# Folding 1/rms into the last down group's activations, and moving the norm's ones-products behind other products

## The chip, the core and the metric

One core of a Trainium2 chip runs the whole program. Its engines run side by side, each with a queue of its own that is worked off in order: TensorE (PE, with the weight loads as PEld), VectorE (DVE), ScalarE (ACT), GpSimd (POOL) and SyncE (SP, which issues most loads). The metric is the device time of one execution in microseconds, as the median of several runs. TensorE's clock has two levels, 1.2 and 2.4 GHz, and the profile's granted clock says which share of the full one a stretch had.

## What is computed

A two-layer encoder over 512 positions of width 1024, in float32. The reference, cut to what matters here:

```python
for i in range(2):
    h = h + 0.5 * swiglu(rmsnorm(h, ffn1_norm[i]), ...)        # (silu(x Wg) * (x Wu)) Wd, inner width 2816
    u = rmsnorm(h, mix_norm[i]) @ w_in[i]                      # feeds attention, mLSTM, Fourier mixing
    h = h + concat(y_mla, y_mlstm, y_fnet) @ w_out[i]
    h = h + 0.5 * swiglu(rmsnorm(h, ffn2_norm[i]), ...)
    e = rmsnorm(p[i] @ ple_w_proj[i], ple_post_norm[i])        # embedding, 256 wide, per layer
    h = h + sigmoid(rmsnorm(h, ple_gate_norm[i]) @ ple_w_gate[i]) * e
out = rmsnorm(h, final_norm)
```

## The kernel before

The state `h` lies transposed in SBUF as 8 tiles of 128 channels by 512 positions. Every matrix product is made of three TensorE products, since each float32 operand is split into a rounded part and a rest (`mm3`, lines 161 to 163: `xh` or `ah` with `whi`, `xl` or `al` with `whi`, `xh` or `ah` with `wlo`). ScalarE casts the rounded part (L134, L376), VectorE subtracts the rest (L131). Weights arrive in 512 KB tiles through SP's queue.

The factor 1/rms of a norm is not multiplied into the input of a product. `Stage.high` and `Stage.low` (L305, L312) make `xh` and `xl` from `h` times the gain alone and sum the squares on the way (`sqacc`, L199). The factor follows later in two forms: `Norm.tok` (L209) multiplies `sqacc` by a column of ones on TensorE, four small products, and VectorE makes 1/rms from it in a dozen small steps (`rtok`); `Norm.bc` (L245) spreads `rtok` over the partitions with four transposes on TensorE, and ScalarE copies it out as `rbc` (L247). Results are multiplied by `rbc` afterwards.

- **Feed-forward.** The 22 inner tiles `u` are made one after the other; from the fifth on each takes seven smaller products (`p1` to `p7`, a Winograd form over halves of 256 positions). GpSimd multiplies the gate part `g1` (L546) and `g2` (L594) by `rbc`; ScalarE applies silu; `finish` multiplies `g2` by `c22` on GpSimd (L504); `p4` multiplies `g1` on VectorE (L582). The down-projection runs over groups of 5, 4, 4, 4 and 5 inner tiles; the last group's products stand at the end in an order written by hand. `flush` takes a finished output tile: VectorE multiplies it by `rbc` into `qa` (L603) and adds half of that to `h` (L604). In the last group `flush` also makes the next stage's `xh` and `xl`. The order in a feed-forward part is written out by hand on all engines.
- **Mixing.** `tokens` makes 96 products of width 272 (L718 to L720), 12 for each of the 8 channel tiles; `inT` follows with tiles of 512 (24 products each). TensorE's order is that of the program; the others are scheduled.
- **Embedding (`ple`).** 48 projection products (eight tiles `e`, copied out on ScalarE at L1302, squared and summed), then eight gate tiles of 24 products. `post` multiplies the eight `e` by their own norm (L1316). All engines are scheduled. In the second layer the gates are made in two halves of 256 positions, and their raw weights `gr` come through a ring of three buffers of its own (cast to `gh`, rest in `gl`, kept for both halves).

Of the kernel before, what the change touches and what calls it, by code (L numbers as in the profile page):

```python
# [14 lines left out]
ALU = mybir.AluOpType  # L15
# [9 lines left out]
NF = DFF // P  # L25
# [9 lines left out]
GROUPS = (5, 4, 4, 4, 5)  # L35
# [30 lines left out]
CH = {}  # L66
# [27 lines left out]
def trunk(ctx: ExitStack, tc, xT, pT, pos, W, gains, cst, dftc, out):  # L94
# [13 lines left out]
    V, S, G = nc.vector, nc.scalar, nc.gpsimd  # L108
# [219 lines left out]
    def ffn(l, cgu, cd, st, nxt, first=False):  # L328
# [2 lines left out]

        with tc.tile_pool(name="ap", bufs=1) as ap, tc.manual_schedule():
            items, clock = [], [0.0]

# [4 lines left out]
            def tile(tag, bufs, shape, dt=F32):  # L341
                return ap.tile([P] + shape, dt, tag=tag, name=tag, bufs=bufs)
# [4 lines left out]
            def qa():  # L347
                return tile("qa", 4, [T])

            def pw():  # L350
                return tile("pw", 6, [2, T], F32R)

            acts = {}

            def act(f):
# [140 lines left out]
            def small(tag):  # L496
                return tile(tag, 2, [H])

            h1, h2 = slice(0, H), slice(H, T)

            def finish(u):
                d = U[u]
                S.activation(d["g2"], d["g2"], AF.Silu)
                G.tensor_tensor(d["g2"], d["g2"], d["c22"], op=ALU.mult)  # L504
# [58 lines left out]
            def p7(u, after=None):  # L563
                def run():
                    d = U[u]
                    p = d["w", "S3"]
                    product(u, "B", p[:, 0], p[:, 1], "T3", False)
                    d["c22"] = small("c22")
                    S.copy(d["c22"], d["B"])
                    V.scalar_tensor_tensor(d["c22"], d["E"], -1.0, d["c22"], op0=ALU.mult, op1=ALU.subtract)  # L570
                    S.activation(d["g1"], d["g1"], AF.Silu)
                    if after is not None:
                        finish(after)

                return run, load(u, "S3", 0, "A11") + [(7.0, lambda: parts(u, "S3"))]
# [23 lines left out]
            pys = {}  # L599

            def flush(m, last):
                y = qa()
                V.tensor_tensor(y, pys.pop(m), st.rb, op=ALU.mult)  # L603
                V.scalar_tensor_tensor(h[:, m], y, 0.5, h[:, m], op0=ALU.mult, op1=ALU.add)  # L604
                if last:
                    nxt.high(m)
                    if m:
                        nxt.low(m - 1)
                    if m == NK - 1:
                        nxt.low(m)  # L610
# [51 lines left out]
            u, n = NF - 1, GROUPS[g]  # L662
# [21 lines left out]
    def mix(l, st, nxt):  # L684
        with tc.tile_pool(name="mp", bufs=1) as mp, tc.manual_schedule(engines={mybir.EngineType.PE}):
# [12 lines left out]
            def inT(i, tag="ps"):  # L698
                wh, wl = stream(l, CH["inT"] + i)
                pt = bank(tag)  # L700
                blocks(pt, wh, wl, st)
                return pt
# [4 lines left out]
            def tokens(first, n, width, after=()):  # L707

                per = -(-NK // n)
                pns = [bank() for _ in range(NT)]  # L710
                for k in range(NK):
                    if k % per == 0:
                        wh, wl = stream(l, first + k // per, width * min(per, NK - k))
                    b = slice((k % per) * width, (k % per + 1) * width)
                    for c in range(NT):
                        ts = slice(c * P, (c + 1) * P)
                        xh, xl, pn = st.hi[k][:, ts], st.lo[k][:, ts], pns[c][:, 0:width]
                        mm(pn, xh, wh[:, b], start=k == 0, stop=False)  # L718
                        mm(pn, xh, wl[:, b], start=False, stop=False)  # L719
                        mm(pn, xl, wh[:, b], start=False, stop=k == NK - 1)  # L720
                    if k in after:
                        after[k]()
                return pns
# [2 lines left out]
            V.memset(va[:, :, :, 64:65], 1.0)  # L726
            g16 = mp.tile([P, NT, 16], F32, name="g16")
            o = l * GW + _G["ifb"][0]
            pns = tokens(CH["inN"], 3, 272, {3: st.tok, 6: st.bc})
            pmx = [inT(j, "pm") for j in range(2)]  # L730
            for c in range(NT):
                V.scalar_tensor_tensor(g16[:, c], pns[c][:, 256:272], st.rt[:, c:c + 1], gv[:, o:o + 16],
                                       op0=ALU.mult, op1=ALU.add)
# [50 lines left out]
            qa, qb = t2("qa"), t2("qb")  # L784
# [67 lines left out]
            for j in range(2):  # L852
# [4 lines left out]
                for i in (0, 1, 3, 4):  # L857
                    a, b = max(0, 2 - i), T - max(0, i - 2)
# [25 lines left out]
            def maps(j):  # L884
# [12 lines left out]
                for c in range(NT):  # L897
# [10 lines left out]
            pns = tokens(CH["inF"], 2, 256, {3: lambda: rqs.append(nq.tok(st.rt)),  # L908
                                             6: lambda: rqs.append(nq.bc(rqs[0], MLA_SCALE))})
# [200 lines left out]
            kqs, qr, vs, probs, turned, pys = [], [], [], {}, {}, {}  # L1110
# [167 lines left out]
    def ple(l, st, nxt):  # L1278


        with tc.tile_pool(name="pp", bufs=2) as pp:
            raw = wp.tile([P, 2 * T], F32, tag="wraw", name="wraw", bufs=2)
            nc.sync.dma_start(raw, pT[l])
            ph = wp.tile([P, 2 * T], F32R, tag="whi", name="whi")
# [5 lines left out]
            for m in range(NK):  # L1290
                if m % 4 == 0:
                    wj = stream(l, CH["proj"] + m // 4)
                pe = bank("pm" if m % 2 else "ps")
                for j in range(2):
                    b = slice((2 * (m % 4) + j) * P, (2 * (m % 4) + j + 1) * P)
                    mm3(pe, wj[0][:, b], wj[1][:, b], ph[:, j * T:(j + 1) * T], pl[:, j * T:(j + 1) * T], j == 0, j == 1)
                if m == 3:
                    st.tok()
                if m == 6:
                    st.bc()  # L1300
                e = pp.tile([P, T], F32, tag="e", name="e", bufs=NK)
                S.copy(e, pe)  # L1302
                nm.add(e)
                es.append(e)
# [8 lines left out]
            def post(r):  # L1313
                rb = nm.bc(r)
                for i in range(NK):
                    V.scalar_tensor_tensor(es[i], es[i], gcol(l, "post", i), rb, op0=ALU.mult, op1=ALU.mult)  # L1316

            if nxt is not None:
                pgs = []
                for m in range(NK):  # L1320
                    gh, gl = stream(l, CH["gate"] + m)
                    pgs.append(bank("pm" if m % 2 else "ps"))
                    blocks(pgs[m], gh, gl, st)
                    if m == 0:
                        r = nm.tok()
                    if m == 1:
                        post(r)
                    for i in ((), (0, 1), (m,))[min(m, 2)]:
                        gate(i, pgs[i], slice(0, T))
                        nxt(i)  # L1330
                return
# [34 lines left out]
            for b in range(2):  # L1366
                pgs = []
                acc = pp.tile([P, T // 2], F32, tag="acc", name="acc")
                accs.append(acc)
                for m in range(NK):  # L1370
                    if b == 0:
                        raw = pp.tile([P, CHUNK], F32, tag="gr", name="gr", bufs=3)
                        nc.sync.dma_start(raw, W[l, CH["gate"] + m])
                        gw.append((pp.tile([P, CHUNK], F32R, tag="gh", name="gh", bufs=NK),
                                   pp.tile([P, CHUNK], F32R, tag="gl", name="gl", bufs=NK)))
                        split(*gw[m], raw)
                    pgs.append(bank("pm" if m % 2 else "ps")[:, 0:T // 2])
                    for k in range(NK):
                        kb = slice(k * P, (k + 1) * P)
                        mm3(pgs[m], gw[m][0][:, kb], gw[m][1][:, kb], st.hi[k][:, half[b]], st.lo[k][:, half[b]],  # L1380
                            k == 0, k == NK - 1)
                    if b == 0 and m == 1:
                        r = nm.tok()
                    if b == 0 and m == 2:
                        post(r)
                    if b == 1 and m == 2:
                        final_tok(0)
                    if b == 1 and m == 4:
                        final_out(0)
                    for i in ((), (), (0, 1, 2), (m,))[min(m, 3)]:  # L1390
                        gate(i, pgs[i], half[b])
                        sq = acc if i == 0 else pp.tile([P, T // 2], F32, tag="sq", name="sq")
                        S.activation(sq, h[:, i, half[b]], AF.Square)
                        if i < NK - 1:
                            S.activation(h[:, i, half[b]], h[:, i, half[b]], AF.Copy, scale=fg(i))
                        if i >= NK - 2:
                            sqs[b].append(sq)
                        elif i:
                            V.tensor_tensor(acc, acc, sq, op=ALU.add)
# [6 lines left out]
    st = stage(0, "ffn1")  # L1406
# [12 lines left out]
    for l in range(L):  # L1419
# [4 lines left out]
        st = stage(l + 1, "ffn1") if l + 1 < L else None  # L1424
# [132 lines left out]
```

## Time and profile before

| | us |
|---|---|
| median of 3 runs | 2092.74 (2091.53 to 2094.8) |
| profiled execution | 2091.12 |
| its span | 2089.3 |
| TensorE busy | 2008.6 (96%) |
| VectorE busy | 1567.7 (75%) |
| ScalarE busy | 1016.6 (49%) |
| GpSimd busy | 356.4 (17%) |
| mean granted clock of TensorE | 0.985 |

The span is the part of the execution that the trace covers; 1.8 us of the execution lie outside it. Shares are of the span. An engine counts as busy only for work, not for issuing loads or for waiting on a semaphore.

### The profile page before, as it was taken

The numbers are of one execution on the slowest core, as the hardware profiler recorded it, in microseconds if no ns is written. First come the engines' busy times: TensorE is split into PE (matmuls) and PEld (weight loads), VectorE is DVE, ScalarE is ACT, GpSimd is POOL, SyncE is SP. The second block draws the span as 40 slices with busy tenths as digits, with TensorE's granted clock in tenths as the row PEclk, the third lists the DMA queues.
The fourth block names the chain that finished last, engine by engine and source line by source line (L and its number), as shares of the span: only waits on it lengthen the run. The fifth ranks groups of instructions, "written<-read, shape, count | busy, mean of one in ns | idle before, by whom it ended". The sixth has DMA issues, their size and how long they took to land.

```text
span 2089.3 us, 31724 instructions
## 1 busy us (share of the span) xinstructions
PE 2008.6 (96%) x12216; PEld 1770.4 (85%) x12216; DVE 1567.7 (75%) x2607; ACT 1016.6 (49%) x1938; POOL 356.4 (17%) x415
## 2 busy tenths in 40 slices
PE   7899999999999999999999999999989999999997
PEld 5789999888777899998768999988877878999977
DVE  5687787687856778877867887776786667788777
ACT  3534454456734445445544444454675353444463
POOL 0222232001001232221011322220000022233200
PEclk9899999999999999999999999999999999999999
DMA  4365554221123555562225456522210246555431
GB/s 137 102 171 152 151 151 129 83 81 48 57 71 105 147 140 153 152 162 88 94 81 166 134 145 169 152 88 87 83 54 21 91 125 170 145 153 139 138 112 50
DMA packets 96664, 244.23 MB, mean 117 GB/s; under 512 B 10592, under 2 KB 14064, under 8 KB 96512
## 3 DMA queue, kind: packets, MB, share of 16 engines
q1 hardware_dynamic: 73488, 200.98, 28.9%
q0 software_dynamic: 20784, 37.84, 11.2%
q10 hardware_dynamic: 2240, 3.38, 0.5%
q8 instruction: 96, 1.57, 0.3%
q14 instruction: 56, 0.46, 0.1%
HBM read 240.06 MB, written 2.10 MB: 116 GB/s over the span
## 4 chain that ended last, share of the span: by engine, by line
PE 81%; DVE 8%; ACT 5%; issue 3%; DMA 1%; POOL 0%; DVEq 0%; ACTq 0%; POOLq 0%
PE ps L493 29%; PE ps L162 8%; PE ps L161 8%; PE ps L163 7%; PE pm L161 7%; PE pm L163 7%; PE pm L162 7%; PE pm L493 5%; DVE wlo L131 1%; ACT whi L376 1%; ACT pw L408 1%; DVE tl L131 1%; PE ps L718 1%; DVE xl L312 1%; PE ps L719 1%
## 5 line engine op out<-in xcount | busy, mean ns | idle before, releaser
L493 PE MATMUL ps<-th,pw 128*128 128x256 f32 x2304 | 442.9, 284 | 1.5 <-ACT pw L457 1.0
L131 DVE TENSOR_TENSOR wlo<-wraw,whi 128x1024 fp32r<-128x1024 f32 (+3 forms) x275 | 344.4, 1253 | 130.7 <-ACT whi L376 93.6
L493 PEld LDWEIGHTS ps<-th,pw 128*128 128x128 f32 x2304 | 371.6, 193 | 4.4 <-ACT pw L457 1.7
L493 PE MATMUL ps<-tl,pw 128*128 128x256 f32 x1152 | 327.1, 284 | 0.0
L376 ACT CAST whi<-wraw 128x512 fp32r<-128x512 f32 (+1 forms) x261 | 204.4, 811 | 220.9 <-PE pm L162 118.0
L493 PEld LDWEIGHTS ps<-tl,pw 128*128 128x128 f32 x1152 | 221.8, 192 | 1.1
L131 DVE TENSOR_TENSOR pw<-qd,pw 128x512 fp32r<-128x512 f32 x216 | 172.6, 801 | 9.9 <-ACT pw L457 4.8
L469 POOL DMA_DIRECT2D qd<-in_W x144 | 125.9, 963 | 215.2 <-DMA qd<-in_W 212.7
L161 PE MATMUL pm<-ah,whi 128*128 128x512 f32 x392 | 155.3, 396 | 0.0
L163 PE MATMUL pm<-ah,wlo 128*128 128x512 f32 x392 | 154.6, 394 | 0.0
L162 PE MATMUL pm<-al,whi 128*128 128x512 f32 x392 | 154.2, 393 | 0.0
L559 ACT COPY g<-ps 128x256 f32<-128x256 f32 x72 | 26.8, 373 | 231.8 <-PE ps L493 231.8
L134 ACT CAST whi<-wraw 128x1024 fp32r<-128x1024 f32 (+6 forms) x86 | 81.0, 944 | 119.4 <-PE ps L162 53.1
L161 PE MATMUL ps<-xh,whi 128*128 128x512 f32 x288 | 119.2, 414 | 18.8 <-ACT xh L305 13.6
L457 ACT CAST pw<-qd 128x512 fp32r<-128x512 f32 x216 | 124.3, 616 | 0.0
L134 ACT CAST ah<-g 128x256 fp32r<-128x256 f32 x144 | 56.7, 404 | 137.0 <-DVE g L582 130.3
L161 PE MATMUL ps<-ah,whi 128*128 128x512 f32 x312 | 123.3, 395 | 0.0
L163 PE MATMUL ps<-ah,wlo 128*128 128x512 f32 x312 | 123.0, 394 | 0.0
L162 PE MATMUL ps<-al,whi 128*128 128x512 f32 x312 | 122.7, 393 | 0.0
L131 DVE TENSOR_TENSOR pw<-qa,pw 128x512 fp32r<-128x512 f32 x144 | 108.2, 752 | 16.2 <-ACT pw L457 16.2
L163 PE MATMUL ps<-xh,wlo 128*128 128x512 f32 x288 | 117.0, 406 | 3.3 <-DVE wlo L131 3.2
L162 PE MATMUL ps<-xl,whi 128*128 128x512 f32 x288 | 117.3, 407 | 1.4 <-DVE xl L312 1.3
(389 smaller groups left out, 5187.2 us busy)
## 6 DMA issues: line engine op xcount, KB each, us to landing
wraw<-in_W SPq DMA_DIRECT2D x245, 512.0 KB, 3.4
qd<-in_W SPq DMA_DIRECT2D x216, 256.0 KB, 4.2
qd<-in_W POOLq DMA_DIRECT2D x144, 256.0 KB, 4.5
gr<-in_W SPq DMA_DIRECT2D x8, 512.0 KB, 4.0
wraw<-in_W SPq DMA_DIRECT2D x8, 320.0 KB, 2.8
wraw<-in_dftc SPq DMA_DIRECT2D x4, 516.0 KB, 3.3
h<-in_xT ACTq DMA_DIRECT2D x8, 256.0 KB, 4.4
wraw<-in_W SPq DMA_DIRECT2D x4, 408.0 KB, 3.1
```

The source lines that it names most:

```text
L131: V.tensor_tensor(lo, x, hi.bitcast(F32), op=ALU.subtract)
L134: S.copy(hi, x)
L161: mm(o, wh, xh, start=first, stop=False)
L162: mm(o, wh, xl, start=False, stop=False)
L163: mm(o, wl, xh, start=False, stop=last)
L312: V.scalar_tensor_tensor(xl, h[:, m], self.g(m), self.hi[m].bitcast(F32), op0=ALU.mult, op1=ALU.subtract)
L376: S.copy(hi[:, b], w["raw"][:, b])
L408: S.activation(xg[:, j], h[:, i + 4 * j], AF.Copy, scale=st.g(i + 4 * j))
L457: S.copy(p[:, 0], U[u][src])
L469: nc.gpsimd.dma_start(U[u][name], up[:, T:2 * T] if add == "A22" else gate[:, 0:T], accum_op=ALU.add)
L493: mm(U[u][o], x[:, b], y, start=first and i + j == 0, stop=i == 3 and j == 2, skip_group_check=not first)
L559: S.copy(d["g2"], d["B"])
```

## The change

For the last down group (inner tiles 17 to 21) the up half is scaled too: `p7` multiplies `g1` by `rbc` once more, after silu, and `c22` by `rbc`, both on GpSimd. Their products then carry the factor, and `flush` of the last group adds half of the product to `h` straight from PSUM. In mixing, the ones-products and the transposes leave the loop over the channel tiles: the first stand behind all 96 token products, the second behind the first tile of `inT`. In the embedding, TensorE's order is now the program's; the ones-products of both norms stand behind the first gate tile, and the transposes of both behind the second one (first layer) or the third (second layer).

```diff
@@ in ffn @@
+            LAST = NF - GROUPS[-1]
...
@@ in p7 @@
                     S.activation(d["g1"], d["g1"], AF.Silu)
+                    if u >= LAST:
+                        G.tensor_tensor(d["g1"], d["g1"], st.rb[:, h1], op=ALU.mult)
+                        G.tensor_tensor(d["c22"], d["c22"], st.rb[:, h2], op=ALU.mult)
                     if after is not None:
                         finish(after)
...
             def flush(m, last):
-                y = qa()
-                V.tensor_tensor(y, pys.pop(m), st.rb, op=ALU.mult)
+                y = pys.pop(m)
+                if not last:
+                    py, y = y, qa()
+                    V.tensor_tensor(y, py, st.rb, op=ALU.mult)
                 V.scalar_tensor_tensor(h[:, m], y, 0.5, h[:, m], op0=ALU.mult, op1=ALU.add)
...
@@ in mix @@
-            pns = tokens(CH["inN"], 3, 272, {3: st.tok, 6: st.bc})
-            pmx = [inT(j, "pm") for j in range(2)]
+            pns = tokens(CH["inN"], 3, 272)
+            st.tok()
+            pmx = [inT(0, "pm")]
+            st.bc()
+            pmx.append(inT(1, "pm"))
...
@@ in ple @@
-        with tc.tile_pool(name="pp", bufs=2) as pp:
+        with tc.tile_pool(name="pp", bufs=2) as pp, tc.manual_schedule(engines={mybir.EngineType.PE}):
...
-                if m == 3:
-                    st.tok()
-                if m == 6:
-                    st.bc()
...
                     if m == 0:
+                        st.tok()
                         r = nm.tok()
                     if m == 1:
+                        st.bc()
                         post(r)
-                    for i in ((), (0, 1), (m,))[min(m, 2)]:
+                    for i in ((), (), (0, 1, 2), (m,))[min(m, 3)]:
...
-                    if b == 0 and m == 1:
+                    if b == 0 and m == 0:
+                        st.tok()
                         r = nm.tok()
                     if b == 0 and m == 2:
+                        st.bc()
                         post(r)
```

Three places show what stands in the queues. The first is the end of GpSimd's queue in the first feed-forward part, from the last inner tile's `p2` on. Before:

```order
L546 TENSOR_TENSOR g_3570<-g_3570,rbc 128x256
L594 TENSOR_TENSOR g_3555<-g_3555,rbc 128x256
L504 TENSOR_TENSOR g_3555<-g_3555,c_3587 128x256
L594 TENSOR_TENSOR g_3681<-g_3681,rbc 128x256
L504 TENSOR_TENSOR g_3681<-g_3681,c_3711 128x256
```

And now, where L548, L599 and L506 are the lines 546, 594 and 504 of before, and L575 and L576 are new:

```order
L548 TENSOR_TENSOR g_3576<-g_3576,rbc 128x256
L599 TENSOR_TENSOR g_3561<-g_3561,rbc 128x256
L575 TENSOR_TENSOR g_3576<-g_3576,rbc 128x256
L576 TENSOR_TENSOR c_3719<-c_3719,rbc 128x256
L506 TENSOR_TENSOR g_3561<-g_3561,c_3593 128x256
L599 TENSOR_TENSOR g_3689<-g_3689,rbc 128x256
L506 TENSOR_TENSOR g_3689<-g_3689,c_3719 128x256
```

The two new multiplications for the last inner tile stand ahead of the product of `g2` and `c22` of the tile before it. Each of the five last tiles has such a pair.

The second place is TensorE in the first layer's mixing: token products (272 wide), ones-products, and `inT` (512 wide). Before:

```order
L720 MATMUL ps<-whi,xl 128x272
L209 MATMUL pm<-ones,sqacc 128x1 x4
L718 MATMUL ps<-whi,xh 128x272
...
L245 MATMUL pm<-cs,rtok 128x128 x4
L718 MATMUL ps<-whi,xh 128x272
...
L161 MATMUL pm<-xh,whi 128x512
```

And now, where line 727 is the line 720 of before:

```order
L727 MATMUL ps<-whi,xl 128x272
L209 MATMUL pm<-ones,sqacc 128x1 x4
L161 MATMUL pm<-xh,whi 128x512
...
L163 MATMUL pm<-xh,wlo 128x512
L245 MATMUL pm<-cs,rtok 128x128 x4
```

The ones-products stood behind 48 of the token products (four channel tiles) and the transposes behind 84; now the former have all 96 ahead of them and the latter the 24 of the first `inT` as well.

The third place is ScalarE in the second layer's embedding, from the cast of the third gate weight on (`gh`; a square `sq<-e` belongs to one of the tiles `e`, the last of them to the eighth). Before:

```order
L134 CAST gh<-gr 128x1024
L193 ACTIVATE sq<-e 128x512
L134 CAST gh<-gr 128x1024
L193 ACTIVATE sq<-e 128x512
L1309 ACT_TABLE_LOAD
L1309 ACTIVATE t<-t 128x256
L134 CAST gh<-gr 128x1024
```

And now:

```order
L134 CAST gh<-gr 128x1024
L193 ACTIVATE sq<-e 128x512
L1308 COPY e<-pm 128x512
L134 CAST gh<-gr 128x1024
L193 ACTIVATE sq<-e 128x512
L134 CAST gh<-gr 128x1024
L193 ACTIVATE sq<-e 128x512
L134 CAST gh<-gr 128x1024
L193 ACTIVATE sq<-e 128x512
L134 CAST gh<-gr 128x1024 x2
L247 ACTIVATE rbc<-pm 128x512 x2
L1315 ACT_TABLE_LOAD
```

The square of the eighth tile `e` stood behind four casts of gate weights; now it stands behind six. VectorE's queue has the rests `gl` in the same way between the sums of squares. SP's queue is the same in both programs.

## Rows read from the trace of the kernel before

**Rows 1.** The page: busy time, share of the span and instructions of TensorE.

```profile
PE 2008.6 (96%) x12216; PEld 1770.4 (85%) x12216; DVE 1567.7 (75%) x2607; ACT 1016.6 (49%) x1938; POOL 356.4 (17%) x415
```

**Rows 2.** TensorE's waits by line and releaser: us in total, times, longest us.

```profile
PE ps L161 <- ACT xh L305: 13.6, 4, 6.5
...
PE pm L209 <- DVE sqacc L199: 5.9, 3, 2.3
...
PE ps L718 <- DVE qa L603: 2.2, 2, 1.2
...
PE pm L245 <- DVE rtok L177: 2.0, 1, 2.0
```

**Rows 3.** Timeline of TensorE, mixing, layer 0: start, duration, operation, idle before.

```profile
386.29 0.29 PE L719 MATMUL ps<-wlo,xh 128*128 128x272 f32 x1
...
396.01 1.05 PE L209 MATMUL pm<-ones,sqacc 128*128 128x1 f32 x8 [2.31 <-DVE sqacc L199]
...
404.98 0.40 PE L161 MATMUL pm<-xh,whi 128*128 128x512 f32 x1
```

**Rows 4.** Windows, layer 0: busy by engine, then granted clock, DMA, GB/s.

```profile
397.00:398.00 1.00, 1.00 (x8) 1.00 (x8) 0.80 (x7) 0.00 (x0) 0.00 (x0) 0.84 0.29 115
398.00:399.00 1.00, 1.00 (x7) 1.00 (x6) 0.83 (x6) 0.00 (x0) 0.00 (x0) 0.50 0.00 0
```

**Rows 5.** Windows of mixing, layer 1, columns as in rows 4.

```profile
1418.00:1420.00 2.00, 1.42 (x7) 1.42 (x7) 1.01 (x2) 0.00 (x0) 0.00 (x0) 0.57 0.79 260
1420.00:1422.00 2.00, 2.00 (x10) 2.00 (x10) 1.31 (x10) 0.00 (x0) 0.00 (x0) 0.50 0.01 2
...
1424.00:1426.00 2.00, 2.00 (x14) 2.00 (x13) 0.00 (x0) 0.27 (x1) 0.00 (x0) 0.73 0.00 0
```

**Rows 6.** Timeline of VectorE, layer 0, last step ahead of the ones-products.

```profile
395.28 0.68 DVE L199 TENSOR_TENSOR sqacc<-sqacc,sq 128x512 f32<-128x512 f32 x1
```

**Rows 7.** Timeline, embedding of layer 0: first product, transposes, last gate product; ScalarE behind.

```profile
983.82 0.40 PE L161 MATMUL ps<-whi 128*128 128x512 f32 x1
...
1014.75 0.60 PE L245 MATMUL pm<-cs,rtok 128*128 128x128 f32 x4
...
1045.80 0.39 PE L163 MATMUL pm<-xh,wlo 128*128 128x512 f32 x1
```

**Rows 8.** Timeline of TensorE, embedding of layer 1: first projection, ones, transposes, last gate product.

```profile
2008.57 0.39 PE L161 MATMUL ps<-whi 128*128 128x512 f32 x1
...
2018.45 1.05 PE L209 MATMUL pm<-ones,sqacc 128*128 128x1 f32 x8 [1.22 <-DVE sqacc L199]
...
2025.48 0.38 PE L163 MATMUL ps<-xh,gl 128*128 128x256 f32 x1 [0.26 <-DVE gl L131]
...
2075.01 0.28 PE L163 MATMUL pm<-xh,gl 128*128 128x256 f32 x1
```

**Rows 9.** Timeline of VectorE and ScalarE, same stage: rests and casts of gate weights.

```profile
2028.38 1.22 DVE L131 TENSOR_TENSOR gl<-gr,gh 128x1024 fp32r<-128x1024 f32 x1
...
2030.45 1.21 DVE L131 TENSOR_TENSOR gl<-gr,gh 128x1024 fp32r<-128x1024 f32 x1
...
2034.00 1.05 ACT L134 CAST gh<-gr 128x1024 fp32r<-128x1024 f32 x1 [0.15 <-DMA gr<-in_W]
2036.07 1.05 ACT L134 CAST gh<-gr 128x1024 fp32r<-128x1024 f32 x1 [1.02 <-DMA gr<-in_W]
```

**Rows 10.** Timeline of the end of a feed-forward part, layer 0, four engines.

```profile
357.29 0.42 ACT L571 ACTIVATE g<-g 128x256 f32<-128x256 f32 x1
...
358.09 0.73 POOL L504 TENSOR_TENSOR g<-g,c 128x256 f32<-128x256 f32 x1 [2.95 <-ACT g L503]
361.85 1.66 POOL L594 TENSOR_TENSOR g<-g,rbc 128x256 f32<-128x256 f32 x1 [3.02 <-DVE g L593]
...
365.25 0.42 DVE L131 TENSOR_TENSOR al<-g,ah 128x256 fp32r<-128x256 f32 x1 [2.33 <-ACT ah L134]
...
366.89 0.39 PE L162 MATMUL pm<-al,whi 128*128 128x512 f32 x1
```

## The prediction, made before the changed kernel ran

> **What bounds the kernel now.** I read the busy times first: TensorE works in 96% of the span and VectorE in 75% [rows 1], so an edit pays where TensorE stands idle or runs at its lower clock level, and nowhere else. The list of TensorE's waits says where it stands. Three of its lines lie where the change works: the ones-products wait 5.9 us in all for the sum of squares, the first token products 2.2 us for `flush` to free a PSUM bank, the transposes 2.0 us for `rtok` [rows 2]: 10.1 us together. The windows show that this is not the whole price. Behind the 2.31 us wait of layer 0 [rows 3] the granted clock falls to 0.84 and then to 0.50 [rows 4]; behind the equal wait of layer 1 it stays at 0.50 for longer [rows 5]. So each mixing pays its idle time and then a stretch at half speed.
>
> The sum is made against the profiled execution, 2091.1 us (a span of 2089.3 and 1.8 outside). It lies 1.6 us below the median shown; my number is on the median. A measurement of this kernel can tell about 0.2%, or 4 us, from no change.
>
> **Mixing, layer 0.** From the first token product after the down group (386.29) to the first `inT` product (404.98) 18.7 us pass [rows 3]. The work in them is 96 products at a pitch of 0.126 us (12.1), the ones-products (0.8 at full clock) and the transposes (0.5): 13.4. The other 5.3 are the 2.31 us wait [rows 3], about 1.1 for the bank [rows 2], and 1.7 of half clock (0.16 in the first window, three of 0.50, a rest) [rows 4]. After the change the token products need only `xh` and `xl`. VectorE makes the last sum of squares at 395.28 now, behind eight multiplications of 0.68 us that go [rows 6]; the product that needs the last `xl` comes no earlier than 386.29 + 84 x 0.126 = 396.9, so nothing is waited for. The ones-products come at 398.4, three microseconds after their sum even by the old times, and `rtok` has the 5.6 us of `inT(0)` as cover; without that cover its dozen steps (about 2.4 us) would show. Gain 5.1. The transposes come later, and so does `rbc`, but the next tile in TensorE's queue is `inT(1)`, which needs neither.
>
> **Mixing, layer 1.** The same: waits of 2.3 and 1.2 (the longest of each kind, [rows 2]), and half clock worth 0.7 + 1.0 + 1.0 + 0.5 = 3.2 [rows 5], where the window left out reads as the one before it. Gain 6.7. Floor for both layers, if the half clock comes back from elsewhere: 6.9 instead of 11.8.
>
> **Embedding, layer 0.** With TensorE's order fixed, a product of the projection wants its `wlo` at once, where the scheduler had put the `whi` products first. The weights' split moves up in VectorE's queue by the multiplications that go, so I price it at 0.3 us (bounds 0 and 2), in layer 1 too: -0.6. From the first projection product (983.82) to the transposes' end at 1015.1 TensorE does 108 products of 0.233, two sets of ones-products and two of transposes: 27.5 us in 31.3 [rows 7]. The missing 3.8 are waits for weight casts and gaps. In the change the third gate's weight has two whole gate tiles (11 us) as cover. Against that, both `rtok` chains must be ready when the second gate ends; they run interleaved on VectorE, 24 steps of 0.2 and two weight rests, and may be 0 to 1.5 late. Gain 3.0 (bounds 1 and 6; the upper one if the next stage's first wait, which has half clock behind it, shrinks as well). The last gate product then ends near 1043 instead of 1046.2 [rows 7].
>
> **Embedding, layer 1.** This is the step I trust least. Removed are 1.22 and 1.98 [rows 2, 8], 0.26 [rows 8] and a later 0.42: 3.9 us. Added is a wait for the eighth tile `e`. The second ones-products now stand behind the first gate: 2008.57 + 48 x 0.233 + 24 x 0.12 = 2022.6, and 0.5 for the first four. Their sum needs the last square, which ScalarE does behind six casts of gate weights, and VectorE behind six rests. The sixth weight's load waits for the third's rest, since the ring has three buffers. From a rest to the cast three on takes 2034.00 - 2029.60 = 4.4 and 2036.07 - 2031.66 = 4.4, and both casts waited for the load [rows 9]. In the new order ScalarE reaches the third cast at about 2019.5, its rest ends near 2021.5, the sixth cast comes near 2026, its rest and the sum near 2028. So TensorE stands 4 to 5.5 us; I take 4.7. Idle of 2.3 was followed by half clock in both mixings [rows 4, 5], so I add 2.0. Sum 3.9 - 4.7 - 2.0 = -2.8 (bounds +3.9, if the loads are quicker, and -5). The transposes' `rtok` lies behind more rests, but two gate tiles cover it.
>
> **The last down group.** VectorE loses eight multiplications per part, 32 in all, which no product waits for except the bank above. GpSimd gains ten per part. The place that can hurt is the last one: the two new operations stand ahead of the product of `g2` and `c22`, which starts at 358.09 now; silu of `g1` ends at 357.71, so two operations of 0.73 us delay it to 359.2 or 359.3, by 1.2 [rows 10]. Down this chain hang ScalarE's cast, VectorE's rest, the next `g1`, GpSimd's 1.66 us operation, and the last `al`, which ends at 365.67 and is wanted by TensorE at 366.89 [rows 10]. The slack is 1.2, less a semaphore's hop. I take a stall of 0.2 in each of the four parts: -0.8. Bounds: 0, and 1.9 each (-7.6) if both operations take the 1.66 us of the one that ran beside VectorE.
>
> That row bears on a rule of the Trainium skill, "GPSIMD Engine Reference", sections 4.1 and 8: two-input elementwise work belongs on VectorE, where it is about twice as fast, and GpSimd shares its SBUF interfaces with VectorE. The rows show both halves, 0.73 alone against 1.66 beside VectorE [rows 10]. By the rule alone this part would cost the 7.6 and not 0.8; VectorE is mostly idle in those two microseconds, so I go with 0.73.
>
> **Sum.** 5.1 + 6.7 + 3.0 - 0.8 - 0.6 - 2.8 = 10.6 us. 2091.1 - 10.6 = 2080.5, on the median 2082.
>
> **The rivals.**
> - *No new wait in the last embedding.* If the loads land before ScalarE comes to them, the 3.9 count: 10.6 + 6.7 = 17.3, or 2075. For it: the first three loads start some 7 us earlier, when TensorE's last down product has ended. Against: the ring, above.
> - *GpSimd's pair is slow.* At 1.66 us each the last `al` is late by 1.9 in each part: 10.6 - 6.8 = 3.8, or 2089; halfway, 2085. Against: VectorE's next long operation comes only after the pair.
> - *Half clock stays in mixing*, drawn by another short wait there: 10.6 - 4.9 = 5.7, or 2087.
> - *The gain is used up later.* The change moves `rbc` and the gate chain of mixing behind more of ScalarE's queue (two table loads now stand around `rbc`). If a wait there takes the 5 to 7 us, no change: about 2091.
> - *Slower.* The chain through GpSimd at the end of a feed-forward part, repeated four times: with operations of 1.9 us or more the stall is over 2.3 each, as long as the one that drew half clock in mixing, and costs at least 2.3 + 1.7 = 4.0; four of them are 16 against the 11.4 of all else, so 2097. It decides from 2.9 us per part on.
>
> **How the numbers follow.** My forecast, 2078 to 2086, has 0.50; no new wait 0.14; slow pair, halfway or full, 0.12; half clock in mixing 0.09; used up 0.09; slower 0.06. The range 2073 to 2089 leaves out the last two and the far ends. Faster by over 0.2% means below 2088.5: 0.50 + 0.14 + 0.09 and most of the slow pair, 0.84. Within 0.2%: 0.10. Slower: 0.06.
>
> **What would show it.** In both mixings the lines for the bank and the sum of squares leave the list of waits and the granted clock stays at 1.00. In the last embedding a wait of the ones-products for the sum of squares, 4 to 5.5 us, with half clock behind it. At the end of each feed-forward part a wait for `al` of a few tenths, and GpSimd's new operations at 0.7 to 0.9 us. The next feed-forward part after layer 0's embedding starts about 3 us earlier. I am wrong if the first token products still wait, if the pair takes over 1.2 us each, or if the last embedding shows no wait.

## The result, and the profile after

| us | before | changed |
|---|---|---|
| median of 4 runs | 2093.34 (2091.53 to 2094.8) | 2076.43 (2075.13 to 2078.2) |
| profiled execution | 2091.12 | 2077.32 |
| its span | 2089.3 | 2075.4 |

Faster: ratio 0.9931, 95% interval 0.9918 to 0.9944, or 12 to 17 us. I had said 2082 in a range of 2073 to 2089. The median lies in the range, but below the 2078 to 2086 to which I had given half of the chance. As the runs below show, the reasons hold only in part.

The first line of the profile's page and the list of TensorE's waits of the changed kernel, which answer to [rows 1, 2]:

```profile
PE 2004.2 (97%) x12216; PEld 1771.1 (85%) x12216; DVE 1554.6 (75%) x2575; ACT 1016.9 (49%) x1938; POOL 391.9 (19%) x455
```

```profile
PE ps L161 <- ACT xh L305: 11.8, 4, 6.4
...
PE ps L1178 <- ACT prob L1172: 6.3, 4, 2.1
...
PE pm L209 <- DVE sqacc L199: 4.0, 1, 4.0
```

The waits for the bank (2.2 us before) and for `rtok` at the transposes (2.0) are gone. The waits for the sum of squares are one instead of three, but that one is new and longer. TensorE in mixing, layer 0, answers to [rows 3, 6]; first the timeline of TensorE, then that of VectorE:

```profile
383.26 0.29 PE L725 MATMUL ps<-whi,xh 128*128 128x272 f32 x1
...
395.37 0.95 PE L209 MATMUL pm<-ones,sqacc 128*128 128x1 f32 x8
401.84 0.60 PE L245 MATMUL pm<-cs,rtok 128*128 128x128 f32 x4
```

```profile
386.12 0.69 DVE L199 TENSOR_TENSOR sqacc<-sqacc,sq 128x512 f32<-128x512 f32 x1
```

The ones-products find their sum ready 8.6 us before. Something else matters more: the sum is ready 3.5 us behind the first token product. Even at its old place, behind 48 token products of 0.126 us (6 us), the ones-product would not have waited.

Where the time went is read best by pairing the same instruction in two traces. The table gives its start in the trace named, less its start in that of before (negative is earlier), for kernels that are explained below. The differences from one line to the next are what a stage gained or lost.

| start of | before | changed | fold_only | mix_only | ple_only | fold_copy |
|---|---|---|---|---|---|---|
| first Winograd product, layer 0 | 76.79 | -2.4 | -2.3 | -1.9 | -2.1 | -2.0 |
| last Winograd product of that part | 360.96 | -2.9 | -2.7 | -2.4 | -2.7 | -2.4 |
| first transposes of probabilities, layer 0 | 535.37 | -8.3 | -8.1 | -6.6 | -1.1 | -0.6 |
| a product of the output projection, layer 0 | 582.06 | -6.6 | -6.4 | -3.8 | +0.5 | +0.9 |
| last Winograd product, second part | 958.51 | -5.9 | -5.8 | -4.1 | +0.1 | +0.6 |
| norm behind the first embedding | 1056.32 | -11.0 | -10.7 | -3.6 | +0.3 | +1.1 |
| last Winograd product, third part | 1383.42 | -10.8 | -10.5 | -3.3 | +0.2 | +1.1 |
| first transposes of probabilities, layer 1 | 1559.61 | -17.7 | -17.3 | -7.5 | 0.0 | -0.1 |
| a product of the output projection, layer 1 | 1606.43 | -15.1 | -14.8 | -6.1 | 0.0 | +2.6 |
| last Winograd product, fourth part | 1983.27 | -15.6 | -15.7 | -7.1 | 0.0 | +1.7 |
| last transposes of the program | 2081.19 | -13.8 | -20.0 | -5.8 | +10.3 | +1.6 |

In the changed kernel mixing gains 5.4 and 6.9 us up to the transposes of probabilities, the first embedding 5.1, and the last one loses 1.9. At the transposes of probabilities 1.7 and 2.6 are given back. The 2.4 us at the start are no gain of the change: the program is the same there, and all thirteen other traces, ple_only and fold_copy among them, start 1.1 to 2.6 us earlier than that of before.

### The profile page after: what moved, and what is told of

It is laid out like the page before. It is cut to its first block, busy times and chain, and to the rows that moved or that the text cites. A ratio compares the mean times of both kernels' runs of the same rounds, so it can differ in the third digit from the quotient of the medians.

```text
span 2075.4 us, 31741 instructions
## 1 busy us (share of the span) xinstructions
PE 2004.2 (97%) x12216; PEld 1771.1 (85%) x12216; DVE 1554.6 (75%) x2575; ACT 1016.9 (49%) x1938; POOL 391.9 (19%) x455
## 4 chain that ended last, share of the span: by engine, by line
PE 84%; DVE 6%; ACT 5%; issue 3%; DMA 1%; POOL 0%; DVEq 0%; ACTq 0%; POOLq 0%
PE ps L495 30%; PE ps L161 8%; PE ps L162 8%; PE ps L163 8%; PE pm L161 7%; PE pm L163 7%; PE pm L162 7%; PE pm L495 5%; ACT whi L378 1%; ACT pw L410 1%; DVE tl L131 1%; PE ps L725 1%; PE ps L726 1%; PE ps L727 1%; DVE wlo L131 1%
## 5 line engine op out<-in xcount | busy, mean ns | idle before, releaser
L131 DVE TENSOR_TENSOR wlo<-wraw,whi 128x1024 fp32r<-128x1024 f32 (+3 forms) x275 | 349.3, 1270 | 122.3 <-ACT whi L378 89.5
L561 ACT COPY g<-ps 128x256 f32<-128x256 f32 x72 | 26.8, 373 | 228.1 <-PE ps L495 227.4
```

The source lines that it names most:

```text
L131: V.tensor_tensor(lo, x, hi.bitcast(F32), op=ALU.subtract)
L561: S.copy(d["g2"], d["B"])
```

## The experiments

**The three parts alone: fold_only, mix_only, ple_only.** Each takes one part of the change's diff to the kernel before and leaves the other two.

> Only the fold into the last down group, with the mixing and embedding orders of before. My theory: the lighter flush alone is enough for mixing. In the changed kernel the last sum of squares ended at 386.8, 3.5 us after the first token product, while the 48 token products that stood ahead of the ones-products take 6 us; so both the bank wait and the wait for the sum of squares go, and mixing gains 5.3 and 6.9 us up to the attention part, 2081 to 2085 in all (up to 4.3 may be given back in the attention part). Rival: the moved order is what pays, and the fold alone takes away only the waits for the bank, 1.1 each: about 2091, with the 2.3 us waits still there.

> Only the mixing order is changed. My theory: the waits for the sum of squares (2.31 and 2.33) go with their half clock, the waits for the bank (1.06 and 1.15) stay: 4.0 and 5.5 us, 2084 to 2088. So the gains of fold_only and mix_only overlap and their sum exceeds what both give together. Rival: with VectorE as loaded as before, the wait only moves to a later token product that lacks its xl, and less than 3 us are gained in all: above 2090.

> Only the embedding's order is changed. My theory: the first embedding gains 3.8 us at its last gate product, as in the changed kernel, and the last one loses about 2 through the wait of 4 us for the eighth tile's square and the half clock behind it: 2089 to 2093. Rival: the first embedding's gain came from the fold, which frees VectorE early for the split of the weights; then the projection's third product waits for its wlo at both places, 1 to 2 us each, and the time is 2093 to 2096.

Measured against the kernel before (median 2090.24 in these runs): fold_only 2070.17, ratio 0.9896 (0.9877 to 0.9916); mix_only 2083.74, 0.9963 (0.9952 to 0.9975); ple_only 2102.27, 1.0051 (1.0031 to 1.0071).

The fold alone is faster than the whole change; the two intervals do not overlap. In its list of waits no line names the bank, the sum of squares or the transposes; the top of it reads

```profile
PE ps L161 <- ACT xh L305: 12.0, 4, 6.1
PE ps L494 <- ACT whi L377: 7.6, 3, 4.9
PE ps L1174 <- ACT prob L1168: 6.3, 4, 2.1
```

and in the table its column follows that of the changed kernel within 0.4 us down to the last embedding. There it gains 4.2 where the changed kernel loses 1.9. It went below the 2081 that I had expected, because I had priced the mixing alone; it also has the whole gain of the first embedding, with the scheduler's old order.

The mixing order alone does what its theory says and no more (the time is just under its 2084 to 2088). It gains 4.2 us from the second to the third line of the table. In layer 1 it has gained 5.7 at a product 23 us ahead of the first transposes of probabilities, and 1.6 of that go again before them: the granted clock is 0.50 from 1534.8 to 1538.2. The bank waits are left:

```profile
PE ps L718 <- DVE qa L603: 1.9, 2, 1.0
```

The fixed embedding alone costs 12 us, more than theory and rival had said. The list of TensorE's waits of ple_only, then two waits in the first embedding on the timeline:

```profile
PE pm L209 <- DVE sqacc L199: 10.0, 3, 5.3
...
PE ps L163 <- DVE wlo L131: 6.8, 7, 2.1
```

```profile
986.61 0.50 PE L163 MATMUL ps<-whi,wlo 128*128 128x512 f32 x1 [2.06 <-DVE wlo L131]
...
999.15 0.50 PE L161 MATMUL ps<-xh,whi 128*128 128x512 f32 x1 [1.62 <-ACT whi L134]
```

The third projection product waits 2.06 us for its `wlo`: that is the wait which the scheduler's order had avoided, and which the fold, in the changed kernel, removes. In the first embedding gains and waits cancel (+0.1 to +0.3 in the table), so the rival is right about the cause: the first embedding's gain in the changed kernel comes from the fold. In the last embedding the wait for the eighth tile's square is 5.3 us and the stage loses 10.3.

**fold_copy: the fold with VectorE's work put back.**

```diff
-                y = pys.pop(m)
-                if not last:
-                    py, y = y, qa()
-                    V.tensor_tensor(y, py, st.rb, op=ALU.mult)
+                py, y = pys.pop(m), qa()
+                if last:
+                    V.tensor_scalar(y, py, 1.0, None, op0=ALU.mult)
+                else:
+                    V.tensor_tensor(y, py, st.rb, op=ALU.mult)
```

> fold_only with the eight VectorE operations of the last group's flush put back as copies from PSUM of the same size (nothing is computed by them). My theory: what pays in the fold is that these leave VectorE's queue; with them back, both bank waits (1.1), both waits for the sum of squares (2.3) and the waits in the first embedding return, 2088 to 2093. Rival: the gain of fold_only came from elsewhere, from GpSimd's pair or from the schedule, and 2069 to 2075 stays.

Measured 2092.56, ratio 1.0004 (0.9994 to 1.0013). The waits of before return, line by line:

```profile
PE pm L209 <- DVE sqacc L199: 6.0, 3, 2.3
...
PE ps L163 <- DVE wlo L131: 3.2, 5, 0.9
...
PE ps L725 <- DVE qa L608: 2.1, 2, 1.1
...
PE pm L245 <- DVE rtok L177: 2.0, 1, 2.0
```

Eight copies of about 0.68 us in each of four parts are the whole of the fold's 20 us. And GpSimd's pair, which stays in, costs nothing that can be measured.

One thing does not return with them. In layer 1 the ones-products wait as long as before, but no half clock follows, where [rows 5] have 0.50:

```profile
1419.55 1.05 PE L209 MATMUL pm<-ones,sqacc 128*128 128x1 f32 x8 [2.33 <-DVE sqacc L199]
```

```profile
1420.00:1422.00 2.00, 2.00 (x18) 2.00 (x18) 1.22 (x10) 0.00 (x0) 0.00 (x0) 1.00 0.40 156
```

With the waits of before, fold_copy gets through the token products of layer 1 3.0 us sooner.

**late_sum and ring4: the wait in the last embedding.** First the later place, in the branch of the last layer:

```diff
                     if b == 0 and m == 0:
                         st.tok()
+                    if b == 0 and m == 2:
                         r = nm.tok()
-                    if b == 0 and m == 2:
+                    if b == 0 and m == 4:
                         st.bc()
                         post(r)
...
-                    for i in ((), (), (0, 1, 2), (m,))[min(m, 3)]:
+                    for i in (((), (), (), (), (0, 1, 2, 3, 4), (m,)) if b == 0 else ((), (), (0, 1, 2), (m,)))[min(m, 5 if b == 0 else 3)]:
```

> The changed kernel, with the last embedding's second ones-products behind the third gate tile instead of the first, and the transposes behind the fifth. My theory: the wait of 4.0 us goes and with it the half clock (3.4 us in the trace of the changed kernel): 2069 to 2073. Rival: the first gates now leave PSUM two gate tiles later, TensorE waits for a bank or VectorE's backlog carries to the end, and less than 2 us are gained: 2074 to 2077.

> The changed kernel with four buffers instead of three for the raw gate weights of the last embedding. The prediction put the wait for the eighth tile's square down to the ring of three: by that, the wait of 4.0 us falls under 1.5 us and the time is 2069 to 2073. Rival, from the trace of the changed kernel, where the casts up to the sixth did not wait for their loads: the queue work itself is late, casts and rests between the squares; then the wait stays at 3.6 to 4.4 us and the time at 2074 to 2079.

late_sum: 2071.45, 0.9908 (0.9884 to 0.9932), 5 us below the changed kernel (the intervals just overlap); neither the wait nor the half clock behind it is in its trace. ring4 (`bufs=4` for `gr`): 2078.17, 0.994 (0.9925 to 0.9954), no better than the changed kernel, and the wait is the same:

```profile
2013.48 1.87 PE L209 MATMUL pm<-ones,sqacc 128*128 128x1 f32 x8 [4.07 <-DVE sqacc L199]
```

So the ring was not it. What the eighth sum comes behind is read from the timelines of the changed kernel; VectorE, then ScalarE, then TensorE:

```profile
2006.25 1.23 DVE L131 TENSOR_TENSOR gl<-gr,gh 128x1024 fp32r<-128x1024 f32 x1
2007.40 0.69 DVE L199 TENSOR_TENSOR sqacc<-sqacc,sq 128x512 f32<-128x512 f32 x1
...
2009.20 0.69 DVE L199 TENSOR_TENSOR sqacc<-sqacc,sq 128x512 f32<-128x512 f32 x1
...
2009.88 1.22 DVE L131 TENSOR_TENSOR gl<-gr,gh 128x1024 fp32r<-128x1024 f32 x1
2011.01 0.68 DVE L199 TENSOR_TENSOR sqacc<-sqacc,sq 128x512 f32<-128x512 f32 x1
```

```profile
2008.12 0.63 ACT L193 ACTIVATE sq<-e 128x512 f32<-128x512 f32 x1 [0.38 <-DVE sqacc L199]
...
2009.92 0.63 ACT L193 ACTIVATE sq<-e 128x512 f32<-128x512 f32 x1 [0.23 <-DVE sqacc L199]
2010.81 1.05 ACT L134 CAST gh<-gr 128x1024 fp32r<-128x1024 f32 x1 [0.25 <-DMA gr<-in_W]
```

```profile
2011.75 1.56 PE L209 MATMUL pm<-ones,sqacc 128*128 128x1 f32 x8 [4.02 <-DVE sqacc L199]
```

In this stretch VectorE works without a gap: it alternates a rest of 1.23 and a sum of 0.69, 1.8 us for each tile, and with a single buffer for `sq` each square waits for the sum before it. The first cast that waits for its load is the seventh, behind the last square. By this reading the eighth sum is late because it shares its queue with six weight rests, five of which only later gates want. No run moved these rests, so this cause is read from the queue and not tested.

**pool_double, pool_plus1: how much room GpSimd's pair has.** The changed kernel with two (or one) more multiplications of the same size behind each pair; the products go to an unused tile. But the added operations read `g1`, which VectorE's product of `p4` (L589 in these runs) overwrites.

```diff
+                        for _ in range(2):
+                            G.tensor_tensor(tile("idle", 1, [H]), d["g1"], st.rb[:, h1], op=ALU.mult)
```

> The changed kernel with two more GpSimd multiplications of the same size into an unused tile behind each new pair, so that the pair's cost is doubled. My theory: in the changed kernel the last al ended 1.1 us before TensorE wanted it, so 1.5 us more leave waits of some 0.4 us in each of four parts: 2077 to 2080. Rival: the chain through GpSimd decides, a delay there is paid in full and draws half clock: four times 1.5 to 3.2 us, 2082 to 2089.

> The changed kernel with one more GpSimd multiplication behind each pair, where two more cost 3 us in each feed-forward part, most of it in the loop. Theory: there is little slack left behind the pair, so one costs about 1 us in each part: 2079 to 2083. Rival: one is still hidden and the cost starts with the second: 2075 to 2078.

pool_double 2091.93, 1.0006 (0.9996 to 1.0015): the whole gain is gone, about 3 us in each feed-forward part. pool_plus1 2081.42, 0.9952 (0.9935 to 0.9968): 5 us above the changed kernel by the medians, 4 by the ratios. Its new waits in TensorE's list are one of 0.65 us in each part, 2.6 in all; the rest lies within what the lower clock level takes or leaves between traces of one program (again1 and again2 below). pool_plus1 went by its theory. pool_double went past its rival's 2082 to 2089, and without the half clock that the rival named. In pool_double TensorE's waits name the place, and the longest wait of VectorE for GpSimd the reason:

```profile
PE ps L495 <- ACT g L561: 5.3, 8, 0.9
...
PE ps L495 <- DVE g L600: 3.9, 8, 0.6
```

```profile
DVE g L589 <- POOL idle L578: 31.5, 15, 2.5
```

These are products inside the loop, not those at the end where I had looked for the slack. VectorE's product of `p4` waits until the added operations have read `g1`, and it feeds a cast at the head of ScalarE's queue; behind it stands the copy that frees a PSUM bank (L561), and the next product waits for the bank. In the changed kernel the same product waits for the pair once in each part, 0.95 us, and TensorE waits nowhere for it. So the two runs tell what a later `p4` costs. How much room the pair itself has they do not tell, since the added operations hold up `p4` by reading its tile.

**fold_ups, late_ups: a version that beats both.** TensorE waits 2.05 us for the first softmax (attention's probabilities) in both layers. The up-projection of the third head is taken ahead of the first transposes of probabilities, once on fold_only, once on late_sum:

```diff
             po = None
+            ups(2)
             for i, (hd, c) in enumerate(pairs):
                 turn(hd, c)
...
-                if i in (1, 5):
-                    ups(2 + i // 4)
+                if i == 5:
+                    ups(3)
```

> The fold alone, with the up-projection of the third attention head taken ahead of the first transposes of probabilities, where TensorE waits 2.05 us in both layers and the changed kernel lost 1.6 and 3.4 us to half clock behind it. My theory: 15 products (3.5 us) that need nothing from the softmax fill the wait, 2 us and the half clock are gained in each layer: 2061 to 2066. Rival: the weights of that head are not split yet, the wait moves to the first of the 15 products, and the time stays at 2068 to 2072.

> The same move on top of late_sum (changed kernel, later sum in the last embedding). Theory and rival as for fold_ups: 2062 to 2067, or 2069 to 2073. If fold_ups and this one lie within 2 us, the orders of mixing and embedding, mended, add nothing to the fold.

fold_ups 2063.94, ratio 0.9874 (0.9859 to 0.9889), the fastest here; late_ups 2068.63, 0.989 (0.987 to 0.9909). The three waits at the first transposes (2.05 us and two of 0.2 to 0.3) are filled, and one of 0.8 us at the next head grows to 2.5:

```profile
PE ps L1174 <- DVE prob L1166: 5.0, 2, 2.5
PE ps L1174 <- ACT prob L1168: 2.2, 2, 1.1
```

The two medians lie 4.7 us apart, not within 2, so the comparison that I had meant to draw stays open. late_ups, at 2068.63, fell between its theory and its rival. What the granted clock lacks of the full one, summed over the trace, is 33.9 us in late_ups and 22.6 in fold_ups, and late_ups' start alone is 1.2 us later.

**again1, again2: the clock at an unaltered wait.**

> The changed kernel once more, unaltered, for one look at its clock. The wait of 2.05 us ahead of the first transposes of probabilities drew no half clock in the trace of before, and 1.6 (layer 0) and 3.4 us (layer 1) in that of the changed kernel. Theory: whether it does is a matter of when it falls, not of the change; the wait stays at 2.0 to 2.1 in both layers, and in this trace or the next at least one of the two layers loses an amount that differs by 1.5 us or more. Rival: the change makes the difference, and both traces show 1.6 and 3.4 again.

> As again1, a second look at the unaltered changed kernel, with the same theory and rival.

2075.88 and 2076.88 (one run each). The wait is 2.05 or 2.06 us in both layers of both. Windows of layer 0 in again1, then of layers 0 and 1 in again2, then of layer 0 in the trace of before, with columns as in [rows 4]:

```profile
530.00:532.00 2.00, 1.14 (x4) 0.86 (x5) 1.94 (x5) 1.95 (x4) 0.00 (x0) 0.85 0.16 39
532.00:534.00 2.00, 2.00 (x7) 1.52 (x7) 1.83 (x4) 0.94 (x2) 0.00 (x0) 0.50 0.59 223
534.00:536.00 2.00, 2.00 (x10) 1.69 (x9) 1.17 (x3) 1.27 (x3) 0.00 (x0) 0.80 0.00 0
```

```profile
534.00:536.00 2.00, 2.00 (x6) 1.49 (x6) 1.81 (x4) 1.39 (x3) 0.00 (x0) 0.50 0.80 260
536.00:538.00 2.00, 2.00 (x8) 1.73 (x7) 1.05 (x3) 0.83 (x2) 0.00 (x0) 0.50 0.01 2
538.00:540.00 2.00, 2.00 (x7) 1.54 (x7) 1.17 (x4) 0.43 (x2) 0.00 (x0) 0.64 0.00 0
...
1546.00:1548.00 2.00, 0.33 (x1) 0.14 (x1) 2.00 (x6) 1.98 (x7) 0.00 (x0) 1.00 0.02 4
1548.00:1550.00 2.00, 1.93 (x11) 1.67 (x12) 1.77 (x6) 1.80 (x3) 0.00 (x0) 1.00 0.66 223
```

```profile
540.00:542.00 2.00, 2.00 (x12) 1.69 (x11) 1.83 (x5) 1.23 (x3) 0.00 (x0) 1.00 0.53 209
```

Half clock cost 1.7 and 1.7 us (layers 0 and 1) in again1, 3.4 and 0 in again2, 1.6 and 3.4 in the first trace of the changed kernel, 0 and 0 in that of before. The wait never changed, so what was given back in attention belongs to no edit: ple_only and fold_copy, with the mixing order of before, lose 1.6 and 1.5 at this place in layer 0 as well, and 0 and 2.7 in layer 1.

## Why the prediction was right, and where not

- **Mixing, 5.1 and 6.7.** Measured 5.4 and 6.9. The size is right, the cause is not. I put it down to the moved products; fold_only gains 5.4 and 6.9 with the old order, and mix_only 4.2 and 5.7 with the old flush. The two edits remove the same waits and don't add. On top of the fold the moves are worth under 0.1 us in each layer. In layer 1 the close fit is partly luck: 3.2 of the 6.7 are half clock behind a wait, and fold_copy has that wait without the half clock. By the prediction's own rows the ones-products had 2.4 us behind their sum (398.4 less 395.96), not three.
- **The last down group, -0.8.** The failed step is the sentence that no product waits for the eight multiplications "except the bank above". They stand in VectorE's queue ahead of the sums of squares and of the weight splits of the next stage, and fold_copy shows that four kinds of wait hang on them: for the bank, the sum of squares, `rtok` and `wlo`. The fold is the change's whole gain. The pair itself cost nothing that can be measured, against 0.8. My slack of 1.2 was taken at the end of the part; a later `p4` makes TensorE wait inside the loop first (pool_double).
- **The slow pair** was a rival, with a price of 7.6. The pair took 0.74 and 0.73 us at the end of the first part, and 1.02 and 0.92 in the mean over all twenty, up to 1.26, where I had said 0.7 to 0.9. The price was not paid. In [rows 10] a GpSimd operation of this size takes 0.73 us alone and one of VectorE 0.42. How near the price was stays open, since pool_plus1, with one more operation behind each pair (0.93 us in the mean), cost 4 to 5 us by way of `p4`. A VectorE rest of 1.23 us took 1.70 beside GpSimd; over the trace of the changed kernel such rests take 1.22 us with no GpSimd operation beside them and 1.76 with one (medians of 201 and 54). The Trainium skill, "GPSIMD Engine Reference", section 8, says that the SBUF interfaces are shared with VectorE; the trace agrees, in both directions.

```profile
354.89 0.74 POOL L575 TENSOR_TENSOR g<-g,rbc 128x256 f32<-128x256 f32 x1 [1.90 <-ACT g L573]
355.59 0.73 POOL L576 TENSOR_TENSOR c<-c,rbc 128x256 f32<-128x256 f32 x1
...
359.68 1.70 DVE L131 TENSOR_TENSOR wlo<-wraw,whi 128x1024 fp32r<-128x1024 f32 x1 [0.20 <-ACT whi L378]
```

- **First embedding, +3.0 and -0.6 for the split.** Measured +5.1 and no wait for the split; 3.8 of it lie between the first projection product and the last gate product (61.98 us before, 58.15 now), 1.1 behind that one. The mechanism was wrong: the fixed order gives 0.2 of it (changed kernel against fold_only), the fold the rest; without the fold the order costs a wait of 2.06 us, the upper bound that I had given.
- **Last embedding, -2.8.** Measured -1.9, a wait of 4.02 (4.7 forecast) and half clock of 3.4 (2.0 forecast). The wait was foreseen, its cause was not: ring4 refutes the ring. The price in full is larger than my sum showed, since the fold would have gained 4.2 there: the fixed order costs the change 6.1 us in this stage.
- **Not in the sum:** 1.7 and 2.6 given back in attention, and 2.4 at the start of the program, both chance; they take 1.9 us. The errors above do not cancel: every term came out better than forecast, by 0.3 and 0.2 in mixing, 0.9 in the last down groups, 2.4 and 1.2 in the two embeddings, 5.0 in all. So 13.8 us lie between the two profiled executions, against 10.6. The median came near the 2075 of the rival without a new wait, though that wait was there: that it stayed in the range is owed to the range's width.

## What to carry to other kernels

Test the parts of a change apart before crediting any: two edits that aim at one wait don't add, and here a third edit took back six of twenty microseconds. Work on an engine that is only 75% busy is still on the path when it stands in its queue ahead of what the next stage waits for; ask what is queued behind an operation, not only who reads its result. A fixed order must be given the time at which each sum is really ready, for every stage in which it is used.

## What the runs showed of the hardware

In this kernel, what a short wait of TensorE costs at the lower clock level is a draw. The same wait of 2.05 us with the same neighbours was followed by no half clock, by 1.6 to 1.7 us or by 3.4 us of loss, in different traces of one program (the changed kernel, again1, again2). The 2.33 us wait of mixing, layer 1, was followed by a loss of 3.2 before and by none in fold_copy; I had taken that half clock as certain. Even a wait of 1.42 us in attention, layer 0, has half clock behind it in again2 (1.7 us, from 512.1) and none in again1. The wait of 4.0 us in the last embedding had 3.4 of loss behind it in all three traces of the changed kernel. The Trainium skill, "TensorE: Matmul & The Clock Gate", Part 1, says that the window in which activity is judged is "free-running" and does not restart with a kernel; the different losses behind one wait fit that, and no run here shows the window itself. So single runs of this kernel can differ by 3 us with no edit between them; the four of before lie between 2091.53 and 2094.8.
